# One-core mixer and expert-choice MoE layer: loads of the mLSTM branch moved to the sync queue, x2 transposes moved by one tile

## The chip, the core and the metric

The kernel runs on 1 core of one Trainium2 chip. The metric is the device time of one execution in microseconds; of several executions the median is given.

## What is computed

One layer on 1024 tokens of width 1024. Two token mixers (a Hyena long convolution and an mLSTM) work side by side on the same input; their outputs are projected to the model's width, gated and added, and projected once more. The sum with the residual goes through a router and 16 experts. Cut to what matters here:

```python
def token_mixer(h, ...):
    p = h @ w_in + b_in
    y_a = hyena_branch(p[..., :ML_START], ...)
    y_b, state = mlstm_branch(p[..., ML_START:GATE_START], ...)
    g_a, g_b = jnp.split(jax.nn.sigmoid(p[..., MERGE_START:]), N_BRANCHES, axis=-1)
    y = (g_a * (y_a @ w_branch_hy) + g_b * (y_b @ w_branch_ml)) @ w_out
    return y, state

def reference(x, c, ctx, ...):
    ...
    yx, _ = token_mixer(hx, *mix_params, rows, GRID_W, ctx_state)
    x = x + ada_x[2][:, None, :] * yx
    hx2 = modulate(rmsnorm(x, norm_ffn_g[l]), ada_x[3], ada_x[4])
    x = x + ada_x[5][:, None, :] * expert_choice_ffn(hx2, w_router[l], ...)
    return rmsnorm(x, final_norm_g)
```

## The kernel before, in words

Every f32 product is made from two float32r parts, hi and lo: `mm3` issues three matmuls, hi x hi, hi x lo and lo x hi. `split` makes the parts: a cast on ScalarE gives hi, a subtraction on VectorE gives lo. Nearly all instructions stand at line 98, a helper that records every operation, so they are told apart by the names of their tiles.

The order: input projections, filters and the Hyena transforms, with the gate products between them (generator `gt`, interleaved with `hy` at L1342); the mLSTM branch; the Hyena branch's projection; the output projection with the router; then the MoE. Outside the first part and the MoE a scheduler sets the order on each engine, from the order in the program, from what each instruction waits for and from its own costs. An engine runs its instructions in that order, and a DMA is issued by the engine whose name stands before `dma_start`, in that engine's order too: `S` is ScalarE (ACT), `SY` the sync engine (SP), `G` GpSimd (POOL).

The stage around the first part of the change:

- `load_y` (L1331 to 1338) loads one half of the mLSTM's output (512 tokens, four tiles `yr`, SP, L1336) and splits it into `yb`. The first half is loaded before the last two gate steps (L1341), the second in job 2 of `ml_branch`.
- `ml_branch` (L1350 to 1379) is a generator of 16 jobs: two halves of the tokens by eight blocks of 128 channels. A job takes one weight block `wmr` (512 x 128, loaded once for both halves by the inner `load`, on ScalarE's queue, split into `wmh` and `wml`), 12 matmuls into `ps`, one gate tile `mgb` (loaded from `gb_d`, on ScalarE's queue), a product on VectorE, and a store of the gated tile to `mb_d` (SP, L1379). The weight of job d + 1 is loaded in job d.
- Three of the generator's steps run with the last Hyena inverse transform (`hyE` and `hyO` are its even-bin and odd-bin sums), others with the splits of the Hyena result (`z`) and the loads of the Hyena branch's weights (`load_wb`, `wbr`, SP, L1418).

Then 16 jobs of `hy_mm` and `hy_out`: 12 matmuls from `z` and `wb`, a product with the gate tile `gab` on VectorE, an addition of the mLSTM's tile (from `mb_d`) on GpSimd, and a split into `mg` (cast on ScalarE, subtraction on VectorE). `load_wo` loads and splits the output weights.

The stage around the second part: `wo_tile` makes one tile of 128 tokens by 512 columns with 24 matmuls; VectorE multiplies it by the row `grow` into `y`, and GpSimd (first eight tiles) adds it to the residual `xs`. `fin_T` stores `xs`, sums its squares and transposes it with four matmuls (`ps<-cst,xs`); `fin_L` makes the router's logits from the transposed tile (`plg<-xT,wrs`); `fin_M` finishes a tile of tokens. The loop over 16 tiles puts `fin_T` of tile i - 2 and `fin_L` of tile i - 3 behind tile i, and closes up at tiles 10 and 11:

```python
for j in ((i - 2,) if i < 10 else (8, 9) if i == 10 else (i - 1,)):
    if j >= 0:
        fin_T(j % 8, j // 8)
for j in ((i - 3,) if i < 11 else (8, 9) if i == 11 else (i - 2,)):
    if j >= 0:
        fin_L(j % 8, j // 8)
```

Of the kernel before, what the change touches and what calls it, by code (L numbers as in the profile page):

```python
# [11 lines left out]
F32R = mybir.dt.float32r  # L12
# [91 lines left out]
def layer_kernel(ctx: ExitStack, tc: tile.TileContext, A: dict, out: bass.AP, dbg=None, stop=None):  # L104
    nc = tc.nc
    in_order, pe_order = [True], [False]
    V, S, G = (InOrder(tc, e, in_order) for e in (nc.vector, nc.scalar, nc.gpsimd))
    T = InOrder(tc, nc.tensor, pe_order)
    SY = nc.sync
    A = dict(A)  # L110
# [6 lines left out]
    def phase(st, name, side=None):  # L117

        pool = st.enter_context(tc.tile_pool(name=name, bufs=1, reuse_waits="tile", side=side))

        def alloc(shape, dt=F32, name=None, tag=None, bufs=1):
            return pool.tile(shape, dt, name=name, tag=tag or name, bufs=bufs)
        return alloc

    def ps(name="ps"):
        return pp.tile([128, 512], F32, name=name, tag="ps")

    def w2(shape, dt=F32, name="w"):
        return wk.tile(shape, dt, name=name, tag="w2", bufs=12)
# [4 lines left out]
    def split(hi, lo, src, E=V):  # L134
        S.copy(hi, src)
        E.tensor_tensor(lo, src, hi.bitcast(F32), op=OP.subtract)

    def mm3(o, a, b, start, stop):
        T.matmul(o, a[0], b[0], start=start, stop=False)
        T.matmul(o, a[0], b[1], start=False, stop=False)  # L140
        T.matmul(o, a[1], b[0], start=False, stop=stop)
# [9 lines left out]
    def flat(name):  # L151
        a = A[name]
        n = 1
        for s in a.shape:
            n *= s
        return bass.AP(tensor=a.tensor, offset=a.offset, ap=[[1, n]])
# [16 lines left out]
    gb_d = dr.tile([1024, 1024], F32, name="gb_d")  # L173
# [854 lines left out]
    def interleave(ga, gb, na, nb):  # L1028

        done = 0  # L1030
        for i in range(nb):
            next(gb)
            while done < na and done * nb < (i + 1) * na:
                next(ga)
                done += 1
# [6 lines left out]
    f = flat("b_in")  # L1042
# [101 lines left out]
    p = ps()  # L1144
# [187 lines left out]
    def load_y(n, tiles):  # L1332
        for h in range(4):
            hi, lo = tiles(h)
            t = w2([128, 512], name="yr")
            SY.dma_start(t, y_d[h * 128:(h + 1) * 128, n * 512:(n + 1) * 512])  # L1336
            split(hi, lo, t)
            yb[n, h] = hi, lo

    y0 = [alxl([128, 2, 512], F32R, name="yb0", tag="xl", bufs=4) for _ in range(4)]  # L1340
    load_y(0, lambda h: (y0[h // 2][:, h % 2], y0[2 + h // 2][:, h % 2]))  # L1341
    interleave(gt, hy, 2, 2)  # L1342
    pgw.close()
    sx2.close()
# [3 lines left out]
    alwm = phase(pwm, "wm", side="right")  # L1348

    def ml_branch():  # L1350
        ws = []

        def load():
            d_ = len(ws)
            raw = w2([128, 4, 128], name="wmr")
            S.dma_start(raw, A["w_branch_ml"][0][:, d_ * 128:(d_ + 1) * 128].rearrange("(k p) n -> p k n", p=128))
            if d_ < 2:
                w = [w2([128, 4, 128], F32R, name=f"wm{v}") for v in "hl"]
            else:
                w = [alwm([128, 4, 128], F32R, name=f"wm{v}", bufs=6) for v in "hl"]  # L1360
            split(w[0], w[1], raw)
            ws.append(w)

        load()
        y1 = [al1([128, 4, 512], F32R, name="yb1", tag=f"hx0{v}", bufs=2) for v in range(2)]
        for n in range(2):
            for d_ in range(8):
                yield
                if n == 0 and d_ < 7:
                    load()  # L1370
                if n == 0 and d_ == 2:
                    load_y(1, lambda h: (y1[0][:, h], y1[1][:, h]))
                sg = w2([128, 512], name="mgb")
                S.dma_start(sg, gb_d[d_ * 128:(d_ + 1) * 128, n * 512:(n + 1) * 512])
                p = ps()
                for ct in range(4):
                    mm3(p, [t[:, ct] for t in ws[d_]], yb[n, ct], ct == 0, ct == 3)
                V.tensor_tensor(sg, p, sg, op=OP.mult)
                SY.dma_start(mb_d[d_ * 128:(d_ + 1) * 128, n * 512:(n + 1) * 512], sg)  # L1379
        yield  # L1380

    mlj = ml_branch()
    next(mlj)
    for _ in hyena_inv1(3):
# [62 lines left out]
    def load_wo(k, dst, c0):  # L1447
        raw = w2([128, 512], name="wor")
        SY.dma_start(raw, A["w_out"][0][k * 128:(k + 1) * 128, c0:c0 + 512])
        split(dst[0], dst[1], raw)  # L1450
# [25 lines left out]
    for i in range(16):  # L1476
        p = ps()
# [12 lines left out]
    def wo(v, k, m):  # L1490
        if m == 0:
            return woA[v][k // 4][:, k % 4]
        return woB[0][v][:, k] if k < 4 else woB[1][2 * v + (k - 4) // 2][:, k % 2]
# [7 lines left out]
    def wo_tile(tt, m):  # L1501
        n, ts_ = tt // 4, slice((tt % 4) * 128, (tt % 4 + 1) * 128)
        p = ps()
        for k in range(8):
            mm3(p, (mg[n][0][:, k, ts_], mg[n][1][:, k, ts_]), (wo(0, k, m), wo(1, k, m)), k == 0, k == 7)
        ms_ = slice(m * 512, (m + 1) * 512)
        y = w2([128, 512], name="y")
        V.tensor_tensor(y, p, grow2[:, ms_], op=OP.mult)
        (V if m else G).tensor_tensor(xs[tt][:, ms_], xs[tt][:, ms_], y, op=OP.add)
# [10 lines left out]
    def fin_T(tt, q):  # L1520

        xq = xs[tt][:, q * 512:(q + 1) * 512]
        G.dma_start(acc_d[tt * 128:(tt + 1) * 128, q * 512:(q + 1) * 512], xq)
        S.activation(w2([128, 512], BF16, name="junk"), xq, AF.Square, accum_out=ssq[:, q, tt:tt + 1])
        p = ps()
        for k in range(4):
            T.transpose(p[:, k * 128:(k + 1) * 128], xq[:, k * 128:(k + 1) * 128], ident)
        t = w2([128, 4, 128], name="xT")
        V.tensor_copy(t, p.rearrange("p (k c) -> p k c", k=4))
        xTs[tt, q] = t  # L1530
# [3 lines left out]
    def fin_L(tt, q):  # L1534

        if q == 1:
            ss = sm([128, 1], name="ss")
            V.tensor_tensor(ss, ssq[:, 0, tt:tt + 1], ssq[:, 1, tt:tt + 1], op=OP.add)
            fin[tt] = [rsqrt(ss, 1, 1.0 / D)]
        if (tt // 4, q) not in plg:  # L1540
            plg[tt // 4, q] = ps("plg")
        pl = plg[tt // 4, q][:, (tt % 4) * 128:(tt % 4 + 1) * 128]
        for k in range(4):
            T.matmul(pl[32 * k:32 * k + 32, :], wrs[:, q * 4 + k, :], xTs[tt, q][:, k], start=True, stop=True,
                     tile_position=(0, 32 * k))
        if q == 0:
            if tt % 4 == 3:
                S.copy(plh[:, tt - 3:tt + 1].rearrange("p t n -> p (t n)"), plg[tt // 4, q])
            return
        pls = w2([128, 128], name="pls")  # L1550
        V.tensor_tensor(pls, pl, plh[:, tt], op=OP.add)
        fin[tt].append(pls)

    def fin_M(tt):

        rs, pls = fin[tt]
        pt = ps("plT")
        T.transpose(pt[:, 0:128], pls, ident)
        V.tensor_reduce(lg[:, tt, :], pt[:, 0:128].rearrange("p (k e) -> p e k", k=4)[:, 0:16], axis=AX.X, op=OP.add)
        V.scalar_tensor_tensor(lg[:, tt, :], lg[:, tt, :], rs, rb, op0=OP.mult, op1=OP.add)  # L1560
        for h in range(2):
            xn = al([128, 512], name="xn", bufs=2) if tt < 7 else w2([128, 512], name="xn")
            xq = xs[tt][:, h * 512:(h + 1) * 512]
            if tt < 7:
                S.activation(xn, xq, AF.Identity, scale=rs)
            else:
                G.tensor_scalar(xn, xq, rs, None, op0=OP.mult)
            G.dma_start(xn_d[tt * 128:(tt + 1) * 128, h * 512:(h + 1) * 512], xn)

    for q in range(2):  # L1570
        for tt in range(8):
            wo_tile(tt, q)
            if q == 0:
                load_wo(tt, (wo(0, tt, 1), wo(1, tt, 1)), 512)
            i = q * 8 + tt
            for j in ((i - 2,) if i < 10 else (8, 9) if i == 10 else (i - 1,)):
                if j >= 0:
                    fin_T(j % 8, j // 8)
            for j in ((i - 3,) if i < 11 else (8, 9) if i == 11 else (i - 2,)):
                if j >= 0:  # L1580
                    fin_L(j % 8, j // 8)
            if i > 10:
                fin_M(i - 11)
# [30 lines left out]
    p = ps()  # L1614
# [27 lines left out]
    p = ps()  # L1642
# [294 lines left out]
    for tt in range(8):  # L1937
# [5 lines left out]
        for n in range(2):  # L1943
            p = held[tt][n] if on_pe else ps()
# [38 lines left out]
```

## Time and profile before

| what | value |
|---|---|
| median of 3 executions | 2316.33 us (2315.45 to 2320.44) |
| the profiled execution's own time | 2321.04 us |
| its span (first to last instruction) | 2319.3 us |
| mean granted TensorE clock | 0.968 |
| TensorE busy | 2178.2 us, 94% |
| VectorE busy | 1685.9 us, 73% |
| ScalarE busy | 1247.6 us, 54% |
| GpSimd busy | 443.2 us, 19% |
| HBM traffic | 260 GB/s over the span |

All stages lie in one span on one core. The shares are means over stages with different limits, so the stages are looked at one by one. In the trace, PE is TensorE, PEld its loading of weights, DVE is VectorE, ACT ScalarE, POOL GpSimd and SP the sync engine; a q behind the name (ACTq, SPq) is the engine's issuing of DMAs. The granted clock is given as a share of full speed.

### The profile page before, as it was taken

The numbers are of one execution on the slowest core, as the hardware profiler recorded it, in microseconds if no ns is written. First come the engines' busy times: TensorE is split into PE (matmuls) and PEld (weight loads), VectorE is DVE, ScalarE is ACT, GpSimd is POOL, SyncE is SP. The second block draws the span as 40 slices with busy tenths as digits, with TensorE's granted clock in tenths as the row PEclk, the third lists the DMA queues.
The fourth block names the chain that finished last, engine by engine and source line by source line (L and its number), as shares of the span: only waits on it lengthen the run. The fifth ranks groups of instructions, "written<-read, shape, count | busy, mean of one in ns | idle before, by whom it ended". The sixth has DMA issues, their size and how long they took to land. (4 is left out here: it accounts for less than half of the span.)

```text
span 2319.3 us, 28323 instructions
## 1 busy us (share of the span) xinstructions
PE 2178.2 (94%) x10609; PEld 1773.5 (76%) x10609; DVE 1685.9 (73%) x1863; ACT 1247.6 (54%) x1398; POOL 443.2 (19%) x382
## 2 busy tenths in 40 slices
PE   6989999999999998899559999999999999999996
PEld 3679887787778787677348888888888888888884
DVE  5784445654447767554778888988898998888897
ACT  2441342324532222222347777777777778777774
POOL 3553101111124534042300111000111000111001
PEclk9879999999999999999779999999999999999998
DMA  7243335555563333864659999999999999999993
GB/s 262 92 133 96 114 111 176 177 191 193 176 203 108 123 110 102 271 222 144 240 194 377 384 385 380 376 395 381 384 384 381 378 386 388 378 388 384 380 350 142
DMA packets 234792, 605.17 MB, mean 261 GB/s; under 512 B 17722, under 2 KB 89462, under 8 KB 231456
## 3 DMA queue, kind: packets, MB, share of 16 engines
q1 hardware_dynamic: 210224, 545.15, 64.0%
q0 software_dynamic: 12128, 41.43, 5.7%
q10 hardware_dynamic: 12304, 16.80, 2.1%
q8 instruction: 83, 1.36, 0.2%
q14 instruction: 53, 0.43, 0.1%
HBM read 539.34 MB, written 63.98 MB: 260 GB/s over the span
## 5 line engine op out<-in xcount | busy, mean ns | idle before, releaser
L98 DVE TENSOR_TENSOR el<-er,eh 128x2048 fp32r<-128x2048 f32 x383 | 874.5, 2290 | 115.7 <-ACT eh L98 106.6
L98 ACT CAST eh<-er 128x2048 fp32r<-128x2048 f32 x384 | 733.7, 1915 | 237.0 <-PE pup L98 170.5
L98 PE MATMUL pup<-eh,xgh 128*128 128x512 f32 x1024 | 319.6, 393 | 1.6 <-ACT xgh L98 1.6
L98 PE MATMUL pup<-eh,xgl 128*128 128x512 f32 x1024 | 316.7, 390 | 0.0
L98 PE MATMUL ps<-hx,whi 128*128 128x512 f32 x960 | 305.8, 399 | 0.0
L98 PE MATMUL pup<-el,xgh 128*128 128x512 f32 x1024 | 274.8, 390 | 0.0
L98 PEld LDWEIGHTS pup<-eh,xgl 128*128 128x128 f32 x1024 | 192.7, 188 | 40.9 <-DVE xgl L98 0.2
L98 PEld LDWEIGHTS pup<-el,xgh 128*128 128x128 f32 x1024 | 192.8, 188 | 40.4
L98 PEld LDWEIGHTS pup<-eh,xgh 128*128 128x128 f32 x1024 | 190.5, 189 | 40.4 <-ACT xgh L98 2.0
L98 PEld LDWEIGHTS ps<-hx,whi 128*128 128x128 f32 x960 | 179.0, 190 | 40.4 <-ACT nt L98 0.8
L98 POOL DMA_INDIRECT acc_d<-ye,idxc x15 | 50.8, 3390 | 747.5 <-DVE ye L98 747.5
L98 PE MATMUL ps<-hx,wlo 128*128 128x512 f32 x480 | 190.2, 396 | 0.0
L98 PE MATMUL acc<-eh,gh 128*128 128x512 f32 x512 | 161.5, 396 | 0.2 <-ACT gh L98 0.2
L98 PE MATMUL acc<-eh,gl 128*128 128x512 f32 x512 | 160.3, 394 | 0.0
L98 PE MATMUL acc<-el,gh 128*128 128x512 f32 x512 | 139.6, 394 | 0.0
L98 PEld LDWEIGHTS acc<-eh,gl 128*128 128x128 f32 x512 | 96.1, 188 | 22.9 <-DVE gl L98 0.4
L98 PEld LDWEIGHTS acc<-el,gh 128*128 128x128 f32 x512 | 96.1, 188 | 22.7
L98 PEld LDWEIGHTS acc<-eh,gh 128*128 128x128 f32 x512 | 95.0, 188 | 21.5 <-ACT gh L98 0.5
L98 PEld LDWEIGHTS ps<-hx,wlo 128*128 128x128 f32 x480 | 90.7, 189 | 21.3
L98 PE MATMUL pg<-hx,gwh 128*128 128x512 f32 x320 | 101.0, 397 | 3.4 <-ACT gwh L98 3.4
L98 ACT ACTIVATE pb<-ps,colv 128x512 f32<-128x512 f32 (+1 forms) x44 | 29.3, 666 | 130.0 <-PE ps L98 122.3
L98 POOL DMA_INDIRECT xg<-xn_d,idxc x16 | 44.9, 2805 | 260.6 <-PE ps L98 226.4
(374 smaller groups left out, 3399.5 us busy)
## 6 DMA issues: line engine op xcount, KB each, us to landing
er<-in_w_exp_dram SPq DMA_DIRECT2D x384, 1024.0 KB, 7.5
wada<-in_w_ada_dram SPq DMA_DIRECT2D x24, 1024.0 KB, 4.9
wraw<-in_w_in_dram SPq DMA_DIRECT2D x30, 512.0 KB, 3.6
K_d<-fk SPq DMA_DIRECT2D x32, 256.0 KB, 2.2
Kt<-K_d SPq DMA_DIRECT2D x16, 512.0 KB, 4.3
v1c<-v_d SPq DMA_DIRECT2D x20, 256.0 KB, 7.6
gwr<-in_w_in_dram SPq DMA_DIRECT2D x20, 256.0 KB, 6.3
eo_d<-eost POOLq DMA_DIRECT2D x16, 256.0 KB, 6.8
```

The source lines that it names most:

```text
L98: r = op(*a, **k)
```

## The change

1. The helper `load_wm` is taken out of `ml_branch`, and the weights are issued on the sync queue. Two loads stand ahead of the last two gate steps (one before the loads of the first half of y, one after), the third at the branch's start, then one per job: two jobs ahead instead of one.
2. The gate tiles `mgb` are loaded on the sync queue too.
3. The second half of y is loaded in job 4 instead of job 2.
4. In the output projection's loop, `fin_T` and `fin_L` stand one tile later (i - 3 and i - 4) up to the closing tiles, where three are made together.

```diff
+    ws = []
+
+    def load_wm():
+        d_ = len(ws)
+        if d_ == 8:
+            return
+        raw = w2([128, 4, 128], name="wmr")
+        SY.dma_start(raw, A["w_branch_ml"][0][:, d_ * 128:(d_ + 1) * 128].rearrange("(k p) n -> p k n", p=128))
...
+    load_wm()
     y0 = [alxl([128, 2, 512], F32R, name="yb0", tag="xl", bufs=4) for _ in range(4)]
     load_y(0, lambda h: (y0[h // 2][:, h % 2], y0[2 + h // 2][:, h % 2]))
+    load_wm()
     interleave(gt, hy, 2, 2)
...
     def ml_branch():
...
-        load()
+        load_wm()
         y1 = [al1([128, 4, 512], F32R, name="yb1", tag=f"hx0{v}", bufs=2) for v in range(2)]
         for n in range(2):
             for d_ in range(8):
                 yield
-                if n == 0 and d_ < 7:
-                    load()
-                if n == 0 and d_ == 2:
+                if n == 0:
+                    load_wm()
+                if n == 0 and d_ == 4:
                     load_y(1, lambda h: (y1[0][:, h], y1[1][:, h]))
                 sg = w2([128, 512], name="mgb")
-                S.dma_start(sg, gb_d[d_ * 128:(d_ + 1) * 128, n * 512:(n + 1) * 512])
+                SY.dma_start(sg, gb_d[d_ * 128:(d_ + 1) * 128, n * 512:(n + 1) * 512])
...
-            for j in ((i - 2,) if i < 10 else (8, 9) if i == 10 else (i - 1,)):
+            for j in ((i - 3,) if i < 10 else (7, 8, 9) if i == 10 else (i - 1,)):
                 if j >= 0:
                     fin_T(j % 8, j // 8)
-            for j in ((i - 3,) if i < 11 else (8, 9) if i == 11 else (i - 2,)):
+            for j in ((i - 4,) if i < 11 else (7, 8, 9) if i == 11 else (i - 2,)):
                 if j >= 0:
                     fin_L(j % 8, j // 8)
```

The scheduler turns this into another order on the engines. On SP, around the loads of the first half of y, where the mLSTM branch begins (`gwr` is the last gate weight; lines of the changed kernel with a +):

```order
 L1174 DMA gwr<-in_w_in_dram 128x4x128 x2
+L1347 DMA wmr<-in_w_branch_ml_dram 128x4x128
 L1336 DMA yr<-y_d 128x512 x4
-L1379 DMA mb_d<-mgb 128x512
-L1336 DMA yr<-y_d 128x512 x2
-L1379 DMA mb_d<-mgb 128x512
-L1336 DMA yr<-y_d 128x512 x2
```

Before, the first half of y is followed by the first store, and the second half of y stands around the second store. Now a weight stands ahead of y, and what follows the four y loads on SP is this, up to the second half of y:

```order
L1347 DMA wmr<-in_w_branch_ml_dram 128x4x128 x3
L1378 DMA mgb<-gb_d 128x512
L1347 DMA wmr<-in_w_branch_ml_dram 128x4x128
L1378 DMA mgb<-gb_d 128x512
L1383 DMA mb_d<-mgb 128x512
L1347 DMA wmr<-in_w_branch_ml_dram 128x4x128
L1378 DMA mgb<-gb_d 128x512
L1347 DMA wmr<-in_w_branch_ml_dram 128x4x128
L1383 DMA mb_d<-mgb 128x512
L1378 DMA mgb<-gb_d 128x512
L1422 DMA wbr<-in_w_branch_hy_dram 128x512 x2
L1383 DMA mb_d<-mgb 128x512
L1347 DMA wmr<-in_w_branch_ml_dram 128x4x128
L1336 DMA yr<-y_d 128x512
L1383 DMA mb_d<-mgb 128x512
L1336 DMA yr<-y_d 128x512 x3
```

Five weights are issued before the first store, the eighth behind the third store, and the second half of y behind the third and fourth. On ScalarE of the kernel before, the same weights and gate tiles are issued among its casts:

```order
L98 DMA wmr<-in_w_branch_ml_dram 128x4x128
L98 DMA gb_d<-sg 128x512
L98 CAST wmh<-wmr 128x512
L98 DMA wmr<-in_w_branch_ml_dram 128x4x128
L98 CAST wmh<-wmr 128x512
L98 DMA mgb<-gb_d 128x512
L98 DMA wmr<-in_w_branch_ml_dram 128x4x128
L98 DMA mgb<-gb_d 128x512
L98 COPY es<-hyE 128x512
L98 CAST wmh<-wmr 128x512
L98 DMA wmr<-in_w_branch_ml_dram 128x4x128
```

Each of these loads stands behind the cast of the one before it; in the changed kernel ScalarE issues none of them. On TensorE, in the output projection, the first transposes of the kernel before stand behind three tiles, ahead of the fourth (`mg_8200` and `mg_8201` are the hi and lo parts of the first 512 tokens):

```order
L98 MATMUL ps<-woA,mg_8201 128x512
L98 MATMUL ps<-cst,xs 128x128 x4
L98 MATMUL ps<-woA,mg_8200 128x512 x2
L98 MATMUL ps<-woA,mg_8201 128x512
L98 MATMUL ps<-woA,mg_8200 128x512 x2
```

In the changed kernel they stand behind the fourth tile, ahead of the first one of the other 512 tokens (`mg_8202`):

```order
L98 MATMUL ps<-woA,mg_8201 128x512
L98 MATMUL ps<-cst,xs 128x128 x4
L98 MATMUL ps<-woA,mg_8202 128x512 x2
L98 MATMUL ps<-woA,mg_8203 128x512
L98 MATMUL ps<-woA,mg_8202 128x512 x2
```

The transposes moved by 24 matmuls; each later group moved likewise, up to tile 10.

## Rows read from the trace of the kernel before

**Rows 1.** The page's first part: busy time, share, instructions of each engine.

```profile
PE 2178.2 (94%) x10609; PEld 1773.5 (76%) x10609; DVE 1685.9 (73%) x1863; ACT 1247.6 (54%) x1398; POOL 443.2 (19%) x382
```

**Rows 2.** Stretches: us, busy (PE first), clock, DMA share, GB/s; the MoE.

```profile
1189.00:2280.00 1091.00, 1090.72 (x4951) 899.45 (x4952) 973.85 (x572) 849.19 (x663) 96.58 (x30) 1.00 0.99 375
```

**Rows 3.** The same table: mLSTM stage, two parts, next stage's start.

```profile
909.40:974.90 65.50, 52.99 (x209) 42.16 (x210) 31.23 (x49) 17.98 (x30) 0.00 (x0) 0.90 0.75 241
...
931.50:945.30 13.80, 6.88 (x17) 4.98 (x17) 8.95 (x15) 6.22 (x11) 0.00 (x0) 0.63 0.79 242
945.30:974.90 29.60, 29.60 (x131) 24.20 (x130) 12.85 (x20) 4.98 (x8) 0.00 (x0) 1.00 0.88 293
...
975.00:990.00 15.00, 15.00 (x66) 12.10 (x65) 7.40 (x10) 2.91 (x5) 4.26 (x3) 1.00 0.80 256
```

**Rows 4.** TensorE's timeline, mLSTM stage (start, us, work, idle before).

```profile
905.76 3.62 PE L98 MATMUL hyE<-hi,hX 128*128 128x256 f32 x16
914.82 1.22 PE L98 MATMUL ps<-yb,wmh 128*128 128x512 f32 x2 [5.44 <-ACT wmh L98]
...
919.54 3.18 PE L98 MATMUL hyO<-hi,hX 128*128 128x256 f32 x14
922.37 0.82 PE L98 MATMUL ps<-yb,wmh 128*128 128x512 f32 x2
...
936.07 1.22 PE L98 MATMUL ps<-yb,wmh 128*128 128x512 f32 x2 [4.54 <-ACT wmh L98]
939.67 0.80 PE L98 MATMUL ps<-yb,wml 128*128 128x512 f32 x1 [2.38 <-DVE wml L98]
...
974.89 25.31 PE L98 MATMUL ps<-z,wb 128*128 128x512 f32 x108
```

**Rows 5.** ScalarE's timeline and its DMA issues, mLSTM stage.

```profile
914.15 0.62 ACT L98 CAST wmh<-wmr 128x512 fp32r<-128x512 f32 x1 [2.59 <-DMA wmr<-in_w_branch_ml_dram]
914.15 0.39 ACTq L98 DMA_DIRECT2D wmr<-in_w_branch_ml_dram  x1
...
932.03 0.39 ACTq L98 DMA_DIRECT2D wmr<-in_w_branch_ml_dram  x1
...
935.40 0.62 ACT L98 CAST wmh<-wmr 128x512 fp32r<-128x512 f32 x1 [1.75 <-DMA wmr<-in_w_branch_ml_dram]
```

**Rows 6.** The tile wmr: durations in ns (min/median/max).

```profile
L98 ACT CAST wmh<-wmr x8: 617/620/622, 914.1 to 947.1; 128x512 fp32r<-128x512 f32 x8
L98 DVE TENSOR_TENSOR wml<-wmr,wmh x8: 681/685/693, 914.8 to 948.8; 128x512 fp32r<-128x512 f32 x8
```

**Rows 7.** SP's issues of the first half of y.

```profile
882.98 5.31 SPq L1336 DMA_DIRECT2D yr<-y_d  x4
```

**Rows 8.** Landings of yr, of mgb and of mb_d, in this order.

```profile
DMA to landing us min/median/max: 4.2/4.3/4.5
...
DMA to landing us min/median/max: 2.6/3.9/5.2
...
DMA to landing us min/median/max: 2.6/5.2/6.1
```

**Rows 9.** TensorE's timeline, output projection and first transposes.

```profile
1019.59 16.48 PE L98 MATMUL ps<-woA,mg 128*128 128x512 f32 x72
1041.03 1.12 PE L98 MATMUL ps<-cst,xs 128*128 128x128 f32 x4 [4.96 <-POOL xs L98]
1041.80 6.80 PE L98 MATMUL ps<-woA,mg 128*128 128x512 f32 x24
...
1049.32 5.75 PE L98 MATMUL ps<-woA,mg 128*128 128x512 f32 x24
```

**Rows 10.** VectorE, then GpSimd, ahead of the first transposes.

```profile
1034.96 0.69 DVE L98 TENSOR_TENSOR mg<-gab,mg 128x512 fp32r<-128x512 f32 x1 [2.12 <-ACT mg L98]
...
1038.34 0.69 DVE L98 TENSOR_TENSOR mg<-gab,mg 128x512 fp32r<-128x512 f32 x1 [2.08 <-ACT mg L98]
...
1039.71 1.27 POOL L98 TENSOR_TENSOR xs<-xs,y 128x512 f32<-128x512 f32 x1 [2.06 <-DVE y L98]
```

More of the change, by code (lines that the diff above doesn't have):

```diff
@@ L1338, in load_y @@
             yb[n, h] = hi, lo
+    ws = []
[5 more added lines that the diff above has]
+        SY.dma_start(raw, A["w_branch_ml"][0][:, d_ * 128:(d_ + 1) * 128].rearrange("(k p) n -> p k n", p=128))
+        if d_ < 2:
+            w = [w2([128, 4, 128], F32R, name=f"wm{v}") for v in "hl"]
+        else:
+            w = [alwm([128, 4, 128], F32R, name=f"wm{v}", bufs=6) for v in "hl"]
+        split(w[0], w[1], raw)
+        ws.append(w)
+    load_wm()
     y0 = [alxl([128, 2, 512], F32R, name="yb0", tag="xl", bufs=4) for _ in range(4)]
     load_y(0, lambda h: (y0[h // 2][:, h % 2], y0[2 + h // 2][:, h % 2]))
+    load_wm()
     interleave(gt, hy, 2, 2)
@@ L1350, in ml_branch @@
     def ml_branch():
[L1351 to L1362, printed above, removed]
-        load()
+        load_wm()
         y1 = [al1([128, 4, 512], F32R, name="yb1", tag=f"hx0{v}", bufs=2) for v in range(2)]
```

## The prediction, made before the changed kernel ran

> **What bounds the kernel now.** I read the engine totals first, then the table of stages, then TensorE's timeline in the two stages that the diff touches, and last the queues that feed them. TensorE is busy for 2178.2 of 2319.3 us [rows 1], so a change is worth what it takes out of TensorE's remaining 141 us of gaps, or out of matmuls that run at a lowered clock. From 1189 to 2280 us, in the MoE, TensorE is busy 1090.72 of 1091.00 us with DMA at 0.99 [rows 2]. Nothing of the diff stands there; that part comes earlier by whatever is saved before it, and keeps its length. So two stages count: the mLSTM branch (16 jobs of 12 matmuls) and the output projection with the x2 transposes.
>
> **The mLSTM stage before.** The even-bin Hyena matmuls end at 905.76 + 3.62 = 909.38, and the first matmul of the next projection follows the last mLSTM matmul at 974.89 [rows 4]: 65.51 us. In its last part, 945.3 to 974.9, TensorE is never idle and does 131 matmuls in 29.60 us at clock 1.00 [rows 3], 0.226 us each. The stage holds 192 such matmuls (16 x 12), 43.4 us, and 16 odd-bin Hyena ones at (922.37 - 919.54)/14 = 0.202 us [rows 4], 3.2 us. That is **46.6 us of work in 65.51, an excess of 18.9 us**. Three gaps make 5.44 + 4.54 + 2.38 = 12.4 us of it, and all three end with a weight's cast or subtraction (wmh, wml) [rows 4]. The other 6.5 us are mostly matmuls at a lower granted clock: from 931.5 to 945.3 it is 0.63 on average, that is, in part the lower of the two levels (1.2 of 2.4 GHz), and 17 matmuls of that stretch took 6.88 us, 0.405 each [rows 3]; it lies behind the gap that ended at 936.07.
>
> Why are the weights late? Their loads are issued from ScalarE's own instruction stream, where they stand among casts that wait for earlier loads. The second load goes out at 914.15, in the moment in which the first one's cast started after its wait for the DMA; a cast starts 3.4 us after its load's issue (932.03 to 935.40) [rows 5].
>
> **The change, term by term.**
> *Weights on SP's queue, two jobs ahead.* Eight weight and 16 gate issues of some 0.4 us [rows 5] leave ScalarE, which is off the path: nothing by itself. What counts is when they start. The first weight stands ahead of the first-half y loads, which began at 882.98 [rows 7], some 25 us before job 0 needs it. Weights 2 to 4 stand ahead of any mLSTM store. So job 0 can follow the even-bin matmuls at 909.4. From there each job takes 12 x 0.226 = 2.73 us (2.7 in the table's stretch), with the odd-bin matmuls (3.2 us) behind job 0. The eighth weight is the last: it stands behind the third store on SP. Job 2 ends at 909.4 + 3.2 + 8.2 = 920.8; with VectorE's product (as long as a subtraction of the same shape, 0.69, [rows 6]) and an issue of 0.4 the store leaves at 921.9; the weight's issue to cast, cast and subtraction (3.4 + 0.62 + 0.69, [rows 5, 6]) end by 926.6. Job 7 wants it at 909.4 + 3.2 + 19.1 = 931.7: 5.1 us to spare. The gaps and the matmuls at the lower clock behind them go: 18.9 us.
>
> *What is late next: the second half of y.* Its loads move from job 2 to job 4, and in SP's order three of the four stand behind the fourth store (about 924.5). Issues at 0.4 us each, a landing of 4.3 [rows 8], then four casts and subtractions (up to 4 x (0.62 + 0.69) = 5.2, [rows 6]) give 932 to 936, and job 8 starts at 909.4 + 3.2 + 21.8 = 934.4. Bounds of the stall: 0 us if the stores leave without delay, 8 us if a store's landing (5.2 median, [rows 8]) is waited for once more, since SP stands in order. I take 3.5, nearer the lower end, since y's first load stands one store earlier than the others and its pieces are consumed one after the other. **Term A: 65.5 - 46.6 - 3.5 = 15.4 us less**, bounds 10.9 to 18.9.
>
> *Gate loads on SP.* They land within 2.6 to 5.2 us [rows 8] and VectorE's product needs them only when its job ends, and TensorE can go on into other PSUM tiles meanwhile. In the second half they alternate with stores on one queue; at 0.4 us an issue two per job are 0.8 of 2.73 us. Cost nothing, if the stores' waits are short; if they aren't, it is the slower rival below.
>
> *x2 transposes one tile later.* Before, three tiles of the output projection stand between the last hy matmul and the first transposes; they are used up at 1019.59 + 16.48 = 1036.07, and TensorE waits 4.96 us for xs [rows 9]. xs is late because its y product stands on VectorE behind the last mg subtraction (1038.34); the POOL addition then ends at 1039.71 + 1.27 = 1040.98 [rows 10], 21.4 us after the projection's first matmul. The tile behind the wait takes 6.80 us, the next one 5.75 [rows 9]. So the wait is worth 4.96 + 1.05 = **6.0 us**. With four tiles ahead, at 16.48 / 3 = 5.49 us each, the transposes are asked for 22.0 us after the projection's first matmul: 0.6 us later than xs is ready. Bounds 0 and 6.0; I take 6.0, nearer the row, because the mg chain starts from the first hy product and so shifts with the stage. The transposes and logits left out at one place are made up at tile 10 (12 instead of 8), the same number of instructions; from there the tail stands as before. **Term B: 6.0 us less.**
>
> Sum: 15.4 + 6.0 = 21.4. The profiled execution took 2321.04 us, 4.7 above the median 2316.33; it would become 2299.6, the median **2294.9, say 2295.0**.
>
> **The rivals.**
> *DMA paces the stage.* The stage moved 241 x 65.5 = 15.8 MB (the whole stage's GB/s by its length, [rows 3]); less the two weights loaded early (512 x 128 f32, 0.26 MB each) 15.3 MB. In its last stretch it ran 293 GB/s at a DMA share of 0.88. At that rate 15.3 MB want 52 us, a little more than the 50.1 that I forecast; at the 256 GB/s of 975 to 990 [rows 3] they want 59.6. Against it: part of these transfers is for later stages and can slip. Term A is then 5.9 to 13.4; with 5.9 the time is 2316.3 - 11.9 = 2304.
>
> *The router part gives nothing.* The mg chain advances by 3.38 us per job (1034.96, 1038.34, [rows 10]) and not by TensorE's 2.73. If its first gate products come some 6 us late against the hy matmuls, because their loads stand behind a denser queue, xs is late again and term B is 0: 2301.
>
> *Slower: SP runs in lockstep.* SP now carries loads behind stores that wait for TensorE and VectorE. Should the last three weights each wait for a store's landing (6.1 at most, [rows 8], + 0.69 + 0.4 = 7.2 us) instead of a job's 2.7, that is 13.5 us; y late by 8; eight second-half jobs at 0.69 + 0.4 + 0.4 + 2.6 = 4.1 us, a product, two issues and the shortest landing of a gate tile, instead of 2.73: 11. Together 32.5 against the 24.9 us saved (18.9 + 6.0): 2324. It decides from the point at which a weight is cast more than 3.4 + 5.1 = 8.5 us after its issue. For it: the stores wait for VectorE, and SP goes through its issues in order. Against it: no store of before landed later than 6.1. The Trainium skill ("Perfetto Trace Analysis", DMA Optimizations) recommends one engine for input loads and another for stores, which speaks against this change: it puts them on one. No run here shows yet which way that goes; the separate queues of before did not keep the weights from being late.
>
> *The waits only move.* Should the first jobs wait for the same weights because the transfers, not the issues, were late, the stage stays near 65 us and the late y eats the 6 us of term B: 2316. Against it stand the ScalarE rows: the second load was issued at the moment when the first one's cast began [rows 5], so it was the issue that came late. The Trainium skill ("DMA: Bandwidth & Descriptors", Issuing engines are not separate DMA queues) holds that all issuing engines share the same DMA engines and that another issuer saves only issue time, which is usually small. By that rule alone, taken for the whole change, this rival would hold, with some 0.4 us per issue to win; the rows contradict it in so far as an issue that is stuck in an in-order stream costs more than its own duration.
>
> **How the numbers follow.** Forecast 0.62, DMA pace 0.20, no router gain 0.08, slower 0.05, no change 0.05. A measurement of this kernel tells 0.2%, 4.6 us, from no change; the first three cases are all faster by more: faster 0.90, same 0.05, slower 0.05. The range takes in both full terms (18.9 + 6.0 = 24.9, 2291.4, and 1.9 more since the three runs differ by up to 5.0: 2289.5) and, on the other side, DMA pace with most of term B lost (5.9 + 2.4: 2308).
>
> **What would show it.** Right: no wmr issue in ScalarE's rows; job 0 directly behind the even-bin matmuls; the stage near 50 us at clock 1.00, with a small wait on yb at job 8 as its only gap; no wait ahead of the first transposes. Wrong: gaps on wmh or wml again; a DMA share near 1 with several small gaps (DMA pace); a wait on xs as before; mgb waits on VectorE once per job (lockstep); or a MoE part that is longer than before.

## The result and the profile after

The changed kernel takes 2295.13 us, the median of 6 executions (2292.09 to 2298.17), against 2317.99 us of the kernel before in the same comparison (6 executions). The ratio is 0.9896, 95% interval 0.9883 to 0.9909: 21 to 27 us less. The prediction was 2295.0 in a range of 2289.5 to 2308.0. The profiled execution took 2295.03 us with a span of 2293.3, 26.0 less than the span before.

TensorE's busy time fell by 6.2 us for the same 10609 instructions [rows 1], so gaps and matmuls at a lower clock have both gone (in the mLSTM stage, 52.99 us busy became 47.54):

```profile
PE 2172.0 (95%) x10609; PEld 1772.4 (77%) x10609; DVE 1687.1 (74%) x1863; ACT 1246.8 (54%) x1398; POOL 443.5 (19%) x382
```

The table of stretches of the changed kernel, with the columns of [rows 2, 3]: the mLSTM stage behind the even-bin matmuls, the hy jobs, and the MoE.

```profile
908.97:956.51 47.54, 47.54 (x208) 38.93 (x208) 31.29 (x50) 15.73 (x27) 0.00 (x0) 1.00 0.86 272
...
956.51:1001.21 44.70, 44.70 (x194) 36.05 (x192) 20.30 (x32) 10.48 (x18) 16.56 (x11) 1.00 0.76 263
...
1163.46:2254.00 1090.54, 1090.30 (x4951) 899.23 (x4952) 973.73 (x572) 849.12 (x663) 96.57 (x30) 1.00 0.99 375
```

The mLSTM stage took 65.50 us with 52.99 busy at clock 0.90 [rows 3]; it now takes 47.54 us, all busy, at clock 1.00. DMA's share rose from 0.75 to 0.86 without pacing it. The MoE's 4951 matmuls keep TensorE busy as long as before, to 0.4 us [rows 2]. TensorE's timeline, as in [rows 4, 9], shows both edited places:

```profile
905.35 3.62 PE L98 MATMUL hyE<-hi,hX 128*128 128x256 f32 x16
908.61 0.82 PE L98 MATMUL ps<-yb,wmh 128*128 128x512 f32 x2
...
911.60 3.62 PE L98 MATMUL hyO<-hi,hX 128*128 128x256 f32 x16
914.86 0.81 PE L98 MATMUL ps<-yb,wmh 128*128 128x512 f32 x2
...
934.62 0.62 PE L98 MATMUL ps<-yb,wmh 128*128 128x512 f32 x2
...
956.51 44.86 PE L98 MATMUL ps<-z,wb 128*128 128x512 f32 x192
1001.21 21.93 PE L98 MATMUL ps<-woA,mg 128*128 128x512 f32 x96
1022.98 0.60 PE L98 MATMUL ps<-cst,xs 128*128 128x128 f32 x4
1023.33 5.75 PE L98 MATMUL ps<-woA,mg 128*128 128x512 f32 x24
1028.92 0.60 PE L98 MATMUL ps<-cst,xs 128*128 128x128 f32 x4
```

Job 0 follows the even-bin matmuls directly (job 1 starts at 914.86, job 8 at 934.62), no row in the stage carries an idle time, and the first transposes stand behind 96 matmuls (four tiles) and wait for nothing.

Between four matmuls that both traces have, the 26.0 us are these. From the first even-bin matmul to the first z matmul: 974.89 - 905.76 = 69.13 before, 956.51 - 905.35 = 51.16 now, **17.97 less**. From there to the output projection: 44.70 both times. From its first matmul to the first transpose of finished logits (1103.35 before, 1077.76 now): 83.76 before, 76.55 now, **7.21 less**. From there to the MoE's first matmul (1189.04 and 1163.46): 85.69 and 85.70. The rest, 0.8 us, lies ahead of the stage and in the MoE.

### The profile page after: what moved, and what is told of

Same layout as the page of the kernel before. It is cut to its first block, busy times and chain, and to the rows that moved or that the text cites. A ratio compares the mean times of both kernels' runs of the same rounds, so it can differ in the third digit from the quotient of the medians.

```text
span 2293.3 us, 28327 instructions
## 1 busy us (share of the span) xinstructions
PE 2172.0 (95%) x10609; PEld 1772.4 (77%) x10609; DVE 1687.1 (74%) x1863; ACT 1246.8 (54%) x1398; POOL 443.5 (19%) x382
```

## The experiments

All runs are read by the same two lengths, each from the one trace of its kernel, since the stretch ahead of the change differs from one trace to the next (last section): "stage" is the first even-bin matmul to the first z matmul, "stretch" the output projection's first matmul to the first transpose of finished logits, and "wait" TensorE's idle time ahead of the first x2 transposes. Each ratio is to the executions of the kernel before that ran beside it.

The text ahead of the result says that the change loads the weights two jobs ahead, and the expectations below repeat it. By the diff it is three: three loads stand before job 0, and job d issues weight d + 3. In the trace of the change the eighth weight leaves at 922.96, as job 4 begins (923.42), and job 7 wants it. So the kernels that are called "two jobs ahead" in the expectations are "three ahead" here.

| kernel | median us | ratio to before (95%) | stage us | stretch us | wait us |
|---|---|---|---|---|---|
| before | 2317.99 | | 69.13 | 83.76 | 4.96 |
| the change | 2295.13 | 0.9896 (0.9883 to 0.9909) | 51.16 | 76.55 | 0 |
| transposes only | 2313.90 | 0.9977 (0.9967 to 0.9988) | 69.76 | 76.56 | 0 |
| mLSTM part only | 2300.57 | 0.9933 (0.9907 to 0.9959) | 51.18 | 83.14 | 3.04 |
| three ahead, ScalarE issues | 2306.35 | 0.9941 (0.9925 to 0.9958) | 51.17 | 87.47 | 8.03 |
| one ahead, SP issues | 2310.35 | 0.9967 (0.9948 to 0.9986) | 65.54 | 79.33 | 1.93 |
| change, ScalarE issues | 2301.53 | 0.9937 (0.9917 to 0.9957) | 51.17 | 81.45 | 3.09 |
| change, gates on ScalarE | 2303.41 | 0.9940 (0.9920 to 0.9961) | 51.16 | 81.48 | 3.17 |
| change, y in job 6 | 2300.37 | 0.9923 (0.9898 to 0.9948) | 53.30 | 76.55 | 0 |
| change, stores on GpSimd | 2304.48 | 0.9940 (0.9921 to 0.9959) | 51.19 | 77.78 | 1.05 |
| before, grow later | 2329.43 | 1.0043 (1.0016 to 1.0069) | 70.40 | 86.91 | 7.72 |
| change, ScalarE issues, grow later | 2299.50 | 0.9923 (0.9899 to 0.9948) | 51.18 | 77.17 | 0.41 |
| change, grow later | 2294.95 | 0.9897 (0.9874 to 0.9920) | 51.17 | 76.55 | 0 |
| change, y in job 2 | 2297.37 | 0.9914 (0.9891 to 0.9938) | 51.17 | 76.55 | 0 |

The ratios scatter by more than the lengths do: the last kernel has both lengths of the change, and a ratio of 0.9914.

### The two parts, each alone

Only the transposes moved, in the kernel before:

```diff
-            for j in ((i - 2,) if i < 10 else (8, 9) if i == 10 else (i - 1,)):
+            for j in ((i - 3,) if i < 10 else (7, 8, 9) if i == 10 else (i - 1,)):
...
-            for j in ((i - 3,) if i < 11 else (8, 9) if i == 11 else (i - 2,)):
+            for j in ((i - 4,) if i < 11 else (7, 8, 9) if i == 11 else (i - 2,)):
```

> The kernel before with only the x2 transposes and logits one tile later. If the two parts of the change add up, the wait for xs (4.96 us) and the slow tile behind it go and nothing else moves: 6 to 7.5 us less than before (2310 to 2312), the mLSTM stage as long as before (69.1 us from the first even-bin matmul to the first z matmul), the stretch from the output projection's first matmul to the first logits transpose 83.8 -> 76.5 us. Rival: the shift only pays because the mLSTM stage brought the mg chain forward; then xs is waited for again and the gain is under 2 us.

And the changed kernel with those two lines put back:

> The changed kernel with the x2 transposes back where they stood before. If the parts add up: 17 to 19 us less than before (2298 to 2301), mLSTM stage 51.2 us without a gap, the wait for xs again 4 to 6 us. Rival: in the change the router part was worth nothing and the mLSTM stage everything: then 24 to 26 us less than before and no wait for xs.

The first has the stretch of the change (76.56) beside the stage of before, the second the stage of the change (51.18) beside nearly the stretch of before (83.14, with a wait of 3.04 us). The savings from the traces, 7.20 and 17.95 + 0.62, add up to 25.8 against 25.2 in the change: by these lengths the parts are independent. The ratios are coarser: 5.3 and 15.5 us less, 20.8 together (12 to 29 by the ends of their intervals), against 24.1. The rival for each fell; the wait of 3.04 us is shorter than the 4 to 6 us expected.

### Queue or distance

The prediction had blamed ScalarE's queue for the late weights. Two kernels take the two halves of that edit apart; both keep the transposes where they stood. Three jobs ahead, with y in job 4, but on ScalarE (against the changed kernel; the two lines that put the transposes back are left out here):

```diff
-        SY.dma_start(raw, A["w_branch_ml"][0][:, d_ * 128:(d_ + 1) * 128].rearrange("(k p) n -> p k n", p=128))
+        S.dma_start(raw, A["w_branch_ml"][0][:, d_ * 128:(d_ + 1) * 128].rearrange("(k p) n -> p k n", p=128))
...
-                SY.dma_start(sg, gb_d[d_ * 128:(d_ + 1) * 128, n * 512:(n + 1) * 512])
+                S.dma_start(sg, gb_d[d_ * 128:(d_ + 1) * 128, n * 512:(n + 1) * 512])
```

> Two jobs ahead as in the change (y in job 4), but weights and gate tiles issued by ScalarE as before; transposes as before. Theory of the queue (the issues are late because they stand among ScalarE's casts): still at least two gaps on weights, 3 to 9 us less than before. Rival, theory of the distance (one job of 2.7 us is shorter than load, cast and subtraction of 4.7 us, two jobs are longer, whatever engine issues): the gaps go, 14 to 18 us less than before.

One job ahead, with y in job 2, but on SP (against the kernel before):

```diff
-            S.dma_start(raw, A["w_branch_ml"][0][:, d_ * 128:(d_ + 1) * 128].rearrange("(k p) n -> p k n", p=128))
+            SY.dma_start(raw, A["w_branch_ml"][0][:, d_ * 128:(d_ + 1) * 128].rearrange("(k p) n -> p k n", p=128))
...
-                S.dma_start(sg, gb_d[d_ * 128:(d_ + 1) * 128, n * 512:(n + 1) * 512])
+                SY.dma_start(sg, gb_d[d_ * 128:(d_ + 1) * 128, n * 512:(n + 1) * 512])
```

> The kernel before with weights and gate tiles issued by the sync queue, one job ahead and y in job 2 as before; transposes as before. Theory of the queue: 12 to 18 us less than before, at most one gap on a weight. Theory of the distance: gaps of about 4.7 - 2.7 = 2 us on several of the eight weights, so only 3 to 9 us less than before.

TensorE's timeline of the first, three jobs ahead on ScalarE:

```profile
911.77 2.54 PE L98 MATMUL hyE<-hi,hX 128*128 128x256 f32 x11
...
962.94 44.85 PE L98 MATMUL ps<-z,wb 128*128 128x512 f32 x192
1007.63 16.48 PE L98 MATMUL ps<-woA,mg 128*128 128x512 f32 x72
1032.15 1.12 PE L98 MATMUL ps<-cst,xs 128*128 128x128 f32 x4 [8.03 <-POOL xs L98]
```

and of the second, one job ahead on SP, where four gaps stay, with ScalarE's casts and SP's issues of the weights (first and last start):

```profile
918.60 0.73 PE L98 MATMUL ps<-yb,wmh 128*128 128x512 f32 x2 [3.26 <-ACT wmh L98]
931.33 0.50 PE L98 MATMUL ps<-yb,wml 128*128 128x512 f32 x1 [0.17 <-DVE wml L98]
937.44 1.15 PE L98 MATMUL ps<-yb,wmh 128*128 128x512 f32 x2 [3.52 <-ACT wmh L98]
950.88 1.82 PE L98 MATMUL ps<-yb,wmh 128*128 128x512 f32 x4 [2.74 <-ACT wmh L98]
```

```profile
L1356 SPq DMA_DIRECT2D wmr<-in_w_branch_ml_dram x8: 368/384/433, 897.1 to 944.6; - x8
L98 ACT CAST wmh<-wmr x8: 616/619/622, 917.9 to 950.2; 128x512 fp32r<-128x512 f32 x8
```

The earlier loads, with y's later place, give the whole stage, 51.17 us, whichever of the two engines issues; the queue alone gives 3.6 of the 18.0 us (69.13 to 65.54). A job lasts 2.7 us and a weight takes 3.4 + 0.62 + 0.69 = 4.7 us from issue to usable [rows 5, 6], in the queue run up to 7.0 (issued at 944.59, both parts ready at 951.55): one job ahead is too short, three are enough. Two were not tried. In the change the eighth weight is usable at 928.84, 3.0 us before job 7 begins (931.82), about one job's length.

In the queue run the first load left SP at 897.1, 21 us ahead of its cast at 917.9. An early issue is not enough there: the cast has its place in ScalarE's order too, and loading further ahead moves that place as well. Nor is the distance per job all that the first run changed. Its first load stands ahead of the last two gate steps, as in the change. ScalarE's issues of the weights (first and last start), in the kernel before and in the first run:

```profile
L98 ACTq DMA_DIRECT2D wmr<-in_w_branch_ml_dram x8: 390/412/472, 910.9 to 941.5; - x8
...
L98 ACTq DMA_DIRECT2D wmr<-in_w_branch_ml_dram x8: 374/446/583, 895.0 to 927.9; - x8
```

The first weight left 5.1 us behind the first even-bin matmul before, and 16.8 us ahead of it here, so the first gap of before (5.44 us) may have gone by that alone. So the queue theory fell for the stage, since ScalarE's queue does no harm there once the loads are early enough. That earlier first loads and three jobs' distance together are the cure is shown; which of the two closes which gap is not.

The 8.03 us wait ahead of the transposes in the first run was in neither theory. It keeps the saving, 13.7 us by the ratio, below the 14 to 18 that the distance theory expected.

### What the queue is good for

> The whole change, but weights and gate tiles issued by ScalarE. From the run with ScalarE's issues and two jobs ahead: mLSTM stage 51.2 us without a gap, and xs ready some 24.5 us after the output projection's first matmul, against 21.9 us of tiles ahead of the transposes. So a wait for xs of 2 to 4 us comes back with a slower tile behind it: 3 to 5 us slower than the change. Rival: the order of the mg chain came from the place of the transposes, not from the queue: no wait, the same time as the change.

That run is the whole change with the two lines above on ScalarE. The next one puts back only the second of them, the gate tiles:

> The whole change, but the gate tiles mgb issued by ScalarE as before. If the gates are off TensorE's path: mLSTM stage 51.2 us, same time as the change within 2 us. Rival: gates on ScalarE stand behind casts, the products and stores come later, and with them the second half of y and the mg chain: a gap of 1 to 4 us at the second half of y or a wait for xs.

Both keep the stage (51.17, 51.16) and lose most of the router part: a wait of 3.09 and 3.17 us in spite of four tiles, the stretch 4.9 us longer of the 7.2 won. In the run with the gates alone on ScalarE, SP, then VectorE, then TensorE:

```profile
959.03 0.36 SPq L1403 DMA_DIRECT2D grow<-in_b_ada_dram  x1
...
964.16 1.29 DVE L98 TENSOR_TENSOR grow<-grow,growt 128x512 f32<-128x512 f32 x2 [9.31 <-DMA mb_d<-mgb]
965.38 0.68 DVE L98 TENSOR_TENSOR mg<-gab,mg 128x512 fp32r<-128x512 f32 x1
...
1020.95 1.12 PE L98 MATMUL ps<-cst,xs 128*128 128x128 f32 x4 [3.17 <-POOL xs L98]
```

The same place in the change, SP, then VectorE with the end of the mg chain, then GpSimd:

```profile
957.86 0.33 SPq L1403 DMA_DIRECT2D grow<-in_b_ada_dram  x1
...
959.51 0.69 DVE L98 TENSOR_TENSOR gab<-ps,gab 128x512 f32<-128x512 f32 x1 [2.10 <-PE ps L98]
...
963.72 1.29 DVE L98 TENSOR_TENSOR grow<-grow,growt 128x512 f32<-128x512 f32 x2 [3.52 <-DMA grow<-in_b_ada_dram]
964.93 0.69 DVE L98 TENSOR_TENSOR mg<-gab,mg 128x512 fp32r<-128x512 f32 x1
...
1019.06 0.69 DVE L98 TENSOR_TENSOR mg<-gab,mg 128x512 fp32r<-128x512 f32 x1 [2.10 <-ACT mg L98]
...
1020.43 1.29 POOL L98 TENSOR_TENSOR xs<-xs,y 128x512 f32<-128x512 f32 x1 [2.06 <-DVE y L98]
```

VectorE's sum of the row grow stands ahead of the first mg subtraction, and its load is one issue among the stores and gab loads of SP. It left 957.86 - 956.51 = 1.35 us after the first z matmul in the change, and 959.03 - 951.16 = 7.87 us after it with the gates on ScalarE. In the row of the run with the gates alone on ScalarE the releaser is named as a store, but in all eleven kernels with the sum ahead of the chain it starts 5.1 to 6.3 us after its load's issue, and the first mg subtraction 1.2 us behind it. So VectorE waits for the load, the mg chain of 16 jobs starts late, and xs is late with it. The start of the chain (first mg subtraction) against the first z matmul, and xs ready against the output projection's first matmul (the end of TensorE's wait, or where there is none the end of GpSimd's addition), go together, though not one for one, in us:

| kernel | mg chain starts after | xs ready after | tiles ahead | wait |
|---|---|---|---|---|
| one ahead, SP issues | 6.9 | 18.4 | 3 | 1.93 |
| mLSTM part only | 7.4 | 19.5 | 3 | 3.04 |
| before | 8.2 | 21.4 | 3 | 4.96 |
| three ahead, ScalarE issues | 13.1 | 24.5 | 3 | 8.03 |
| transposes only | 9.4 | 20.0 | 4 | 0 |
| the change | 8.4 | 20.5 | 4 | 0 |
| change, stores on GpSimd | 11.4 | 23.0 | 4 | 1.05 |
| change, ScalarE issues | 14.4 | 25.0 | 4 | 3.09 |
| change, gates on ScalarE | 14.2 | 25.1 | 4 | 3.17 |

Three tiles cover 16.5 us and four 21.9; the wait is what is left over (in each row with a wait, GpSimd's addition ends 0.05 or 0.06 us before it does). The second column lies 10.6 to 13.2 above the first, so the start of the chain sets xs only to within some 2.6 us: with the transposes alone moved, the chain starts about 1 us later than before, and xs is ready 1.4 us earlier. For the whole change with ScalarE's issues the forecast held (3 to 5 us slower; 4.9 by the stretch, 6.4 by the medians); for the gates alone the rival did, by its wait for xs.

### Slack and stores

The second half of y two jobs later than in the change:

```diff
-                if n == 0 and d_ == 4:
+                if n == 0 and d_ == 6:
```

> The whole change, but the second half of y loaded in job 6 instead of job 4. In the change the last piece of y was ready about as job 8 began, so there is no slack: two jobs later (5.5 us) give a gap of 3 to 6 us on yb at job 8 and lower-clock matmuls behind it, 4 to 9 us more than the change. Rival: y has slack that the trace hides; then under 1 us.

and in job 2, where it was before:

> The whole change, but the second half of y loaded in job 2 as before. Theory: the loads of y and of the last two weights change places on SP, each still in time: mLSTM stage 51.2 us, the same time as the change within 2 us. Rival: the seventh and eighth weight, now behind y, come late: a gap of 1 to 4 us on a weight at job 6 or 7.

With y in job 6, four small gaps open on yb, 0.96 us together, and the stage grows by 2.1 us, less than expected and more than the rival allowed; no long gap opened, because the pieces of y are consumed one after the other:

```profile
941.91 0.50 PE L98 MATMUL ps<-yb,wmh 128*128 128x512 f32 x1 [0.19 <-DVE yb L98]
...
943.24 0.50 PE L98 MATMUL ps<-yb,wmh 128*128 128x512 f32 x1 [0.22 <-DVE yb L98]
...
944.29 0.50 PE L98 MATMUL ps<-yb,wmh 128*128 128x512 f32 x1 [0.32 <-ACT yb L98]
...
945.02 0.50 PE L98 MATMUL ps<-yb,wmh 128*128 128x512 f32 x1 [0.23 <-DVE yb L98]
```

With y in job 2 the stage is 51.17: by the lengths, that edit of the change is worth nothing, as long as the weights run three jobs ahead. The stores of mb_d, on GpSimd instead of SP:

```diff
-                SY.dma_start(mb_d[d_ * 128:(d_ + 1) * 128, n * 512:(n + 1) * 512], sg)
+                G.dma_start(mb_d[d_ * 128:(d_ + 1) * 128, n * 512:(n + 1) * 512], sg)
```

> The whole change, but the stores of mb_d issued by GpSimd, so that SP carries loads alone. If the stores on SP cost nothing now: mLSTM stage 51.2 us and the same time within 2 us, though the second half of y is issued earlier and has 2 us or more to spare. Rival, the rule that loads and stores belong on different engines: 2 us or more faster. Other rival: GpSimd's issues are slower and the stored tiles come late to the mg chain: a wait for xs, 2 to 5 us slower.

The stage stays (51.19) and the stretch is 1.2 us longer, with a wait of 1.05 us. The Trainium skill ("Perfetto Trace Analysis", DMA Optimizations) says that it may make sense to assign one engine to inputs and another to outputs. In this kernel that gains nothing: without the stores on SP, grow's load left SP 4.20 us after the first z matmul instead of 1.35, and the mg chain started later. By the medians this kernel is some 9 us slower than the change. Its trace gives only 1.3 us of that in the two lengths; its first even-bin matmul comes 9.7 us later (915.03 against 905.35), and why stays open.

### Moving grow away

If the sum of grow sets the start of the mg chain, moving it behind the 16 hy jobs should bring xs forward. The same edit in three kernels (before; the change with ScalarE's issues; the change):

```diff
-    grow2 = gate_row(almg([128, 1024], name="grow2"), 2, SY)
...
         hy_out(p, i)
+    grow2 = gate_row(almg([128, 1024], name="grow2"), 2, SY)
```

> The kernel before, with the row grow loaded and summed behind the 16 hy jobs instead of ahead of them. Theory: the wait for xs comes from VectorE's sum of grow, which stands at the head of the mg chain and waits 3.3 us for its load. Then the mg chain starts 3 to 4.5 us earlier and the wait for xs (4.96 us before) shrinks to 0 to 2 us; the mLSTM stage stays at 69 us; the stretch from the output projection's first matmul to the first logits transpose 83.8 -> 78 to 80 us. Rival: the mg chain is paced by its own 3.4 us per job and the sum of grow lies beside it: wait for xs 4 to 6 us as before.

> The whole change with weights and gate tiles issued by ScalarE, and grow moved behind the hy jobs. Theory: what ScalarE's issues cost is only that grow's load leaves SP 5 us later; with grow out of the way no wait for xs is left and the stretch is 76.5 us as in the change, mLSTM stage 51.2. Rival: the stored tiles themselves are late to the mg chain: a wait of 2 to 4 us stays.

> The whole change, and grow moved behind the hy jobs. TensorE has no wait there in the change, so the same time within 2 us; xs is ready 3 to 4 us earlier against the transposes. Rival: 1 us or more faster, because VectorE's or SP's order behind it improves as well.

In the second the wait shrinks from 3.09 to 0.41 us and the stretch is 77.17; in the third the time is the change's (2294.95), with xs ready 18.5 us after the output projection's first matmul instead of 20.5, 2.0 us earlier where 3 to 4 were expected. In the kernel before, the edit made things worse, and the rows say how. VectorE, then TensorE:

```profile
978.50 0.69 DVE L98 TENSOR_TENSOR woA<-wor,woA 128x512 fp32r<-128x512 f32 x1 [6.83 <-ACT woA L98]
...
1022.76 0.73 DVE L98 TENSOR_TENSOR grow<-grow,growt 128x512 f32<-128x512 f32 x1 [1.24 <-DMA growt<-ada_d]
...
1026.17 0.69 DVE L98 TENSOR_TENSOR grow<-grow,growt 128x512 f32<-128x512 f32 x1 [1.86 <-DMA growt<-ada_d]
...
1042.40 1.12 PE L98 MATMUL ps<-cst,xs 128*128 128x128 f32 x4 [7.72 <-POOL xs L98]
```

The scheduler put another instruction at the head of the chain, a subtraction of woA whose weight also comes over SP, and VectorE waited 6.83 us for that, so that the chain starts 0.8 us later than before; and the sums of grow now interrupt the chain in its middle for 1.24 and 1.86 us more. In the second kernel the head wait on woA is there as well:

```profile
965.60 0.69 DVE L98 TENSOR_TENSOR woA<-wor,woA 128x512 fp32r<-128x512 f32 x1 [8.79 <-ACT woA L98]
```

So my theory was too narrow: it is not grow as such, but whichever instruction that depends on a late SP load stands ahead of the chain in VectorE's order. What the runs show is that xs comes late where the chain starts late or is interrupted; a version that clears the head of the chain altogether wasn't tried. None of these kernels beats the change: by stage and stretch the best two equal it.

## Why the prediction came out right

- **The stage becomes TensorE's own work, 18.9 us of excess go.** Right. 47.54 us all busy at clock 1.00, against 46.6 counted; jobs 1 to 7 take (934.62 - 914.86) / 84 = 0.235 us per matmul where I took 0.226.
- **Term A, 15.4 us, measured 18.0.** The step that was mis-sized is the stall on the second half of y, taken as 3.5 us and measured as 0; against it, the matmuls ran 0.9 us slower than counted. The stall was near. The fourth yb subtraction ends at 931.83 + 1.96 = 933.79, and job 8 starts at 934.62: 0.8 us to spare. ScalarE's casts, then VectorE's subtractions, of the change:

```profile
928.13 0.62 ACT L98 CAST yb<-yr 128x512 fp32r<-128x512 f32 x1
931.18 1.89 ACT L98 CAST yb<-yr 128x512 fp32r<-128x512 f32 x3 [2.43 <-DMA yr<-y_d]
...
931.83 1.96 DVE L98 TENSOR_TENSOR yb<-yr,yb 128x512 fp32r<-128x512 f32 x3 [1.19 <-ACT yb L98]
```

  SP's issues behind it, as in the working (third store, eighth weight, first y, fourth store, three y):

```profile
922.59 0.33 SPq L1383 DMA_DIRECT2D mb_d<-mgb  x1
922.96 0.43 SPq L1347 DMA_DIRECT2D wmr<-in_w_branch_ml_dram  x1
923.51 0.56 SPq L1336 DMA_DIRECT2D yr<-y_d  x1
925.43 0.33 SPq L1383 DMA_DIRECT2D mb_d<-mgb  x1
926.59 1.51 SPq L1336 DMA_DIRECT2D yr<-y_d  x3
```

  I had put the third store at 921.9 and the fourth at 924.5; they left 0.7 and 0.9 us later. The working had y usable between 932 and 936, and my choice of 3.5 us put it past the late end, at 937.9; the casts and subtractions overlap, so the early end was the better one.
- **Why the weights were late.** The mechanism that the prediction gave, ScalarE's queue, does not explain the stage: with the loads three jobs ahead ScalarE's queue does as well (51.17 us), and the move to SP alone is worth 3.6 us there. What counted is how early the loads are issued. The rows that the prediction read stand: the weight of the 4.54 us gap left at 932.03, 3.9 us after job 3 began (928.15), behind casts of y. But such a delay is harmless with enough distance. The predicted time didn't depend on which of the two it was, since the change makes both edits. The distance is three jobs and not two; the sum went by the order on the queue and not by that count. Its eighth weight had 5.1 us to spare and measured 3.0.
- **Gate loads on SP at nothing.** Right for the stage, and incomplete: in this place of the program they are worth 4.9 of the 7.2 us of the router part. With them on ScalarE the grow load leaves SP 6.5 us later against the z matmuls and the wait for xs comes back.
- **Term B, 6.0 us, measured 7.2.** Right in kind. The ground given was that the mg chain shifts with the stage. It does here (it starts 8.4 us after the first z matmul, 8.2 before), but that rests on when grow's load leaves SP, which the prediction did not count: with the gates on ScalarE the same stage is followed by a chain that starts at 14.2. The first transposes are asked for 1022.98 - 1001.21 = 21.8 us after the projection's first matmul, and xs is ready at 20.5 (1020.43 + 1.29): 1.3 us to spare where I had 0.6. Of the 1.2 us that I left out, 0.4 are the four transposes themselves (1041.80 - 1041.03 = 0.77 before [rows 9], 1023.33 - 1022.98 = 0.35 now) and 0.2 a shorter wait ahead of the last logits (1.39 before, 1.17 now); the other 0.6 stays open.
- **DMA paces the stage** (0.20): no. 272 GB/s at a share of 0.86 and no gap.
- **SP in lockstep** (0.05): no. Its sign was a cast more than 8.5 us after the issue; the eighth weight is cast 4.5 us after it (922.96 to 927.50). Landings in the change, of the weights, the gates and the stores (compare [rows 8]); the stores land faster than before, 3.3 instead of 5.2 us in the median:

```profile
DMA to landing us min/median/max: 3.3/3.4/3.5
...
DMA to landing us min/median/max: 3.0/4.0/5.2
...
DMA to landing us min/median/max: 3.0/3.3/4.6
```

- **The waits only move** (0.05): no, though the rule weighed there is partly borne out. The Trainium skill ("DMA: Bandwidth & Descriptors", Issuing engines are not separate DMA queues) makes little of which engine issues; for the stage, with the loads three jobs ahead, the runs agree (51.17 on ScalarE, 51.16 on SP). They differ from it in the router part, 81.45 against 76.55 us: not by the time of an issue, but by when an unrelated load, that of grow, leaves SP (7.0 us after the first z matmul against 1.35).
- That the total came within 0.2 us of the forecast is partly luck: 25.6 us of saving in the trace from the stage's start on, against 21.4 predicted, and a ratio that allows 21 to 27.

## What to carry to other kernels

Compare the time from a load's issue to the usable operand (here 4.7 us) with the work of one step (2.7 us) before looking at queues. One step ahead didn't cover it here, and three did with about a step to spare; then the issuing engine hardly mattered to that loop. Count the steps from the program's order, and not from the name of the edit. When DMA issues are moved between engines, look at what else then stands where on the queues, one stage further on: here, with the loads three jobs ahead, the main thing that the queue decided was when an unrelated row of 4 KB per partition was loaded, which VectorE waited for at the head of a chain some 55 us ahead of the TensorE gap. And where the executions of one kernel differ by as much as the effect, compare lengths between instructions that both traces have.

## What the runs showed that I had not expected

The stretch ahead of the change, in which TensorE runs the same matmuls in the same order in all fourteen kernels, ended between 900.0 us (gates on ScalarE) and 915.0 us (stores on GpSimd) at the first even-bin matmul. Some of it is there early. From 50 to 100 us, and the first projection matmul, in the kernel before with grow later:

```profile
50.00:100.00 50.00, 50.00 (x288) 35.22 (x287) 29.33 (x52) 20.27 (x37) 21.80 (x17) 0.93 0.39 142
```

```profile
159.72 0.39 PE L98 MATMUL pj<-whi,hch 128*128 128x264 f32 x1 [2.22 <-ACT whi L98]
```

and in the change with y in job 6:

```profile
50.00:100.00 50.00, 50.00 (x249) 33.55 (x249) 26.22 (x46) 17.58 (x32) 21.00 (x16) 0.83 0.39 142
```

```profile
166.28 0.39 PE L98 MATMUL pj<-whi,hch 128*128 128x264 f32 x1 [1.48 <-ACT whi L98]
```

TensorE is busy throughout in both, and gets through 288 matmuls at a granted clock of 0.93 in one and 249 at 0.83 in the other; the first projection starts 6.6 us later. That is nearly as large as the router part of this change. Five of the fourteen traces have 0.83 in this stretch, with 249 or 250 matmuls, and these are the five whose first even-bin matmul comes at 910.8 or later; the other nine have 0.86 to 0.93 and come at 900.0 to 908.2. Only one trace of each kernel is kept, so whether this goes with the execution or with the kernel is not shown. That four executions of one kernel (y in job 6) took from 2296.07 to 2304.67 us speaks for the execution. It may be why the ratios scatter by more than the two lengths do; what decides it wasn't tried.
